# Seven half-block products instead of eight in the gate and up matmuls of four feed-forward blocks

## The chip, the core and the metric

The kernel runs on one core of a Trainium2 chip. TensorE (PE, with its weight loads as PEld) multiplies, VectorE (DVE) and ScalarE (ACT) work elementwise, GpSimd (POOL) does a little elementwise work and issues some transfers, and SyncE (SP) issues the others. The metric is the time of one execution in microseconds (us) on the device; lower is better. All inputs and outputs are fp32 in HBM.

## The reference, cut to what matters

Two transformer blocks follow each other on 512 tokens of width 1024 (528 tokens in the first feed-forward block, which has 16 meta tokens ahead). Each block has a feed-forward net, a mixer and a second feed-forward net; this case is about the four feed-forward nets.

```python
D_MODEL, D_FF = 1024, 2816

def rmsnorm(x, g):
    xf = x.astype(jnp.float32)
    y = xf * lax.rsqrt(jnp.mean(xf * xf, axis=-1, keepdims=True) + EPS)
    return (y * g.astype(jnp.float32)).astype(x.dtype)

def swiglu(x, w_in, w_out):
    gu = x @ w_in
    return (jax.nn.silu(gu[..., :D_FF]) * gu[..., D_FF:]) @ w_out

# first block, first net (the other three are alike, two without the outer norm)
h = h + 0.5 * rmsnorm(swiglu(rmsnorm(h, gn[0]), ffn_w_in[i, 0], ffn_w_out[i, 0]), gn[1])
```

## The kernel before, in words

**Numbers as pairs.** Every fp32 operand of a matmul is kept as a high and a low part (`hi`, `lo`, both fp32r). A product is three matmuls: hi by hi, hi by lo, lo by hi (function `mm`, line 366). The hidden state `h` is stored with features on the partitions: 8 blocks of 128 features by 528 tokens. `nh` and `nl` are the two parts of `h` times the norm's gain. The norm's factor per token, `r_bc`, is not in them: it is multiplied in after the matmul, when the result is taken out of PSUM.

**Gates and ups.** The 2816 hidden columns are 22 chunks of 128, done in three parts of 6, 8 and 8 (`PARTS`). A chunk is one `Item` of two units: the gate's weights and the up's weights, each 1024 by 128. `run_mm` runs 2 units x 8 feature blocks x 3 = 48 matmuls of 512 columns (in the first net two slices of 272 and 256 columns, so 96). `Ffn.evac` (lines 481 to 485, `split` at 347 and 348) then makes silu(gate) times up from the two PSUM tiles and stores it as the pair `gh`, `gl`. After each part `Ffn.down` multiplies by the output weights (tile `dn`), adding into `y` (or `h`); the last part's down is joined to the next stage in `Bridge.tail` in the first two nets.

**Weights.** `Weights` has a list of loads (`raws`) and of units to make of them (`subs`). `dma` loads one raw tile of 128x2048 fp32 by SP (line 77): for a chunk the gate's 512 KB and the up's 512 KB. There are two raw tiles. `pump` takes the next unit when a slot is free: ACT casts to fp32r (tile `whi`, line 96), DVE subtracts to get the low part (`wlo`, line 97; in the mixers POOL does it). There are six slots (`w4` with 4, `w2` with 2; four in the third net past its first chunks; in the last net `w4` and four of `wx`). A slot is free again when PE has used it, and a raw tile when its last unit is split.

**Order.** Each engine runs its own instructions strictly in the order in which the build leaves them; semaphores tie the engines together. The build's tile layer may shift neighbouring instructions from the order of the source.

**Rotary tables.** In the third net (`ffn3`), a set of some 25 DVE instructions (`tables`, line 1004) is placed in the middle of part 1; its positions are loaded by POOL at line 1002.

Of the kernel before, what the change touches and what calls it, by code (L numbers as in the profile page):

```python
# [15 lines left out]
P = 128  # L16
# [38 lines left out]

class Weights:


    def __init__(self, nc, raw_pool, raw_ahead):
        self.nc = nc  # L60
        self.raw_pool, self.raw_ahead = raw_pool, raw_ahead
        self.raws, self.subs, self.units = [], [], []
        self.raw_tiles = {}
        self.n_raw = self.n_split = self.n_take = self.n_free = 0
        self.pools = []
        self.lo_engine = nc.vector

    def add(self, loads, subs):
        r = len(self.raws)
        self.raws.append([loads, len(subs)])  # L70
        self.subs.extend((r, s) for s in subs)

    def dma(self, n):
        while self.n_raw < min(n, len(self.raws)):
            t = self.raw_pool.tile([P, 2048], F32, tag="raw", name="raw")
            for dst, src in self.raws[self.n_raw][0]:
                self.nc.sync.dma_start(out=dst(t), in_=src)
            self.raw_tiles[self.n_raw] = t
            self.n_raw += 1

    def pump(self):
        nc = self.nc
        while self.n_split < len(self.subs):
            room = [p for p in self.pools if p[1] > 0]
            if not room:
                break
            slot = max(room, key=lambda p: p[1])
            slot[1] -= 1
            pool = slot[0]
            r, make = self.subs[self.n_split]  # L90
            self.dma(r + 1)
            hi = pool.tile([P, 1024], F32R, tag="whi", name="whi")
            lo = pool.tile([P, 1024], F32R, tag="wlo", name="wlo")
            unit, splits = make(self.raw_tiles[r], hi, lo)
# [20 lines left out]

    def free(self, k):
        for _ in range(k):
            self.units[self.n_free].slot[1] += 1
            self.units[self.n_free] = None
            self.n_free += 1  # L120
        self.pump()

    def open(self, pool, n):
        self.pools.append([pool, n, n])

    def close(self, pool):
# [14 lines left out]
def two_blocks(ctx: ExitStack, tc, d, out):  # L141
# [13 lines left out]
    w4 = ctx.enter_context(tc.tile_pool(name="w4", bufs=4))  # L155
# [19 lines left out]
    def col(i):  # L175
        return vec[:, i:i + 1]
# [25 lines left out]

    def add_down(ap, f0, nf):
# [15 lines left out]
    def add_ffn(g_ap, g0, u_ap, u0, d_ap):  # L219
        for f0, nf in PARTS:  # L220
            for f in range(f0, f0 + nf):
                add_gu(g_ap, g0, u_ap, u0, f)
            add_down(d_ap, f0, nf)

    def add_gates(ap):
# [3 lines left out]
        def make(raw, hi, lo):  # L229
            src, hv, lv = view(raw), grid(hi, KD), grid(lo, KD)  # L230
# [234 lines left out]

    class Ffn:
        def __init__(self, name, half):
            self.cm, self.p = open_pool(name)
            self.half = half
# [6 lines left out]
        def evac(self, f, sl, g, u):  # L476
            t0, n = sl
            r = r_bc[:, t0:t0 + n]
            a = self.p.tile([P, 512], F32, tag="a", bufs=2, name="a")[:, 0:n]
            b = self.p.tile([P, 512], F32, tag="b", bufs=2, name="b")[:, 0:n]  # L480
# [5 lines left out]
            split(cut(self.gh, f, sl), cut(self.gl, f, sl), b)  # L486

# [30 lines left out]
    class Bridge:  # L518
# [24 lines left out]
        def tail(self, hl, nk, sink):  # L543
# [4 lines left out]
            cm, more = open_pool("w8", bufs=2, side="right")  # L548
# [39 lines left out]
    cm_w2, w2 = open_pool("w2", bufs=2)  # L588
# [3 lines left out]
    ffn = Ffn("ffn1", 0.5)  # L592
# [17 lines left out]
    W.open(w4, 4)  # L610
# [49 lines left out]
    for part in range(3):  # L660
        items = ffn.items(part)
        if part == 0:
            run_lead(items[:3], br)
            items = items[3:]
            p = ps("vt")
            pe.transpose(p[:, 0:P], vrow, ident)
            dve.tensor_copy(out=vec[:, 48:P], in_=p[:, 48:P])
            for i in (1, 5):
                g = vec[:, V_GN[i]:V_GN[i] + KD]
                dve.tensor_scalar(out=g, in0=g, scalar1=0.5, scalar2=None, op0=ALU.mult)  # L670
        for it in items:
            run_item(it, AB)
        if part < 2:
            ffn.down(PARTS[part][1], AB, sum_y(part == 0))
# [283 lines left out]
    run_lead(items[:3], br)  # L958
    for part in range(3):
        for it in items[3:] if part == 0 else ffn.items(part):  # L960
            run_item(it, [XF])
        if part < 2:
            ffn.down(PARTS[part][1], [XF], sum_y(part == 0))
# [18 lines left out]
    add_ffn(d["ffn2_w_gate_2"][0], 0, d["ffn2_w_up_2"][0], 0, d["ffn2_w_down_2"][0])  # L982
    br = Bridge(XA, XB, V_GN[5], V_F1)
# [6 lines left out]
    run_lead(items[:3], br)  # L990
    W.close(w2)
    for it in items[3:]:
        run_item(it, [XF])
    cm_t, trig = open_pool("trig", side="right")
# [3 lines left out]
    posi = trig.tile([P, 512], I32, tag="sqTrue", bufs=1, name="posi")  # L998
    sinR = trig.tile([P, SEQ], F32, name="sinR")
    cosR = trig.tile([P, SEQ], F32, name="cosR")  # L1000
    tabM = trig.tile([P, SEQ], F32, name="tabM")
    pool.dma_start(out=posi, in_=d["positions_2"][0].partition_broadcast(P))

    def tables():
        def tmp(tag):
            return ffn.p.tile([P, 512], F32, tag=tag, bufs=1 if tag == "th" else 2, name=tag)
        ang, n, k, z, q = tmp("a"), tmp("a"), tmp("b"), tmp("b"), tmp("th")
# [33 lines left out]
    for part in range(3):
        if part:
            for i, it in enumerate(ffn.items(part)):
                run_item(it, [XF])
                if part == 1 and i == 1:
                    tables()
        ffn.down(PARTS[part][1], [XF], add_h((lambda c: pre_chunk(c, XF, V_MIX, pre)) if part == 2 else None))
# [384 lines left out]
    cm_x, wx = open_pool("wx", bufs=4)  # L1432
    W.open(wx, 4)
    W.pump()
    for part in range(3):
        items = ffn.items(part)
        if part == 0:
            run_first(items[0], items[1], ONE, pre)
            items = items[2:]
        for it in items:  # L1440
            run_item(it, ONE)
        if part < 2:
            ffn.down(PARTS[part][1], ONE, add_h())
# [100 lines left out]
```

## Time and profile before

| what | value |
|---|---|
| median of three runs | 2133.37 us (2132.86 to 2138.08) |
| the profiled execution, its run | 2133.48 us |
| the profiled execution, its span | 2131.7 us |
| TensorE's granted clock over the span | 0.988 of full |
| PE busy, share of the span | 97% |
| DVE, ACT, POOL busy | 60%, 38%, 8% |
| HBM read | 180.20 MB, 87 GB/s over the span |

The span is the time from the first to the last instruction of the profiled execution; the run's own time lies 1.8 us above it. Busy time of PE is modelled from pipelined matmuls, so what counts is the time between starts. An engine that is off the chain of waits costs nothing while it idles.

### The profile page before, as it was taken

What the parts mean: (1) busy time and instruction counts of PE and PEld (TensorE: products, weight loads), DVE (VectorE), ACT (ScalarE), POOL (GpSimd) and SP (SyncE); (2) the same over time, 40 slices, a digit from 0 to 9 for tenths busy, and PEclk for the clock granted to TensorE, in tenths of its full rate; (3) what the DMA queues carried; (4) which work ended last, traced back from release to release, by engine and by line L of the source; (5) the groups of instructions that cost most, each with busy time, mean ns of one, the idle gap of its engine ahead of it and who ended that gap; (6) DMA issues with size and microseconds to landing.
All of it is one profiled execution on the core that took longest, in us unless ns stands there. A gap on an engine that the chain in (4) does not pass through costs nothing.

```text
span 2131.7 us, 29589 instructions
## 1 busy us (share of the span) xinstructions
PE 2073.6 (97%) x12047; PEld 1816.5 (85%) x12047; DVE 1278.3 (60%) x2217; ACT 813.7 (38%) x1365; POOL 161.5 (8%) x162
## 2 busy tenths in 40 slices
PE   8999999989999999999999999998999999999998
PEld 8999999988889988888998888887777778888888
DVE  6545345787886734444674653557888875454454
ACT  5333223335455433223342332334666643222222
POOL 0000000025440000000000000003222100000000
PEclk9999999989999999999999999999999999999999
DMA  5232322213322233223322333323212143333311
GB/s 160 92 110 80 100 85 86 70 55 90 95 80 86 64 109 99 91 88 99 93 82 78 99 99 99 99 82 92 56 41 65 40 132 105 100 99 99 99 60 40
DMA packets 285422, 186.32 MB, mean 87 GB/s; under 512 B 6332, under 2 KB 281527, under 8 KB 285287
## 3 DMA queue, kind: packets, MB, share of 16 engines
q1 hardware_dynamic: 282630, 176.15, 27.4%
q0 software_dynamic: 2096, 7.05, 1.0%
q8 instruction: 94, 1.54, 0.3%
q10 hardware_dynamic: 560, 1.24, 0.2%
q14 instruction: 42, 0.34, 0.0%
HBM read 180.20 MB, written 4.23 MB: 87 GB/s over the span
## 4 chain that ended last, share of the span: by engine, by line
PE 83%; DVE 10%; ACT 4%; issue 2%; POOL 1%; DMA 0%; ACTq 0%; POOLq 0%; DVEq 0%; SPq 0%
PE acc L366 46%; PE dn L366 24%; PE accB L366 3%; PE accA L366 3%; PE wo L366 2%; DVE accF L909 1%; PE p L301 1%; PE ro L1318 1%; ACT whi L96 1%; DVE cv L770 1%; DVE wlo L97 1%; PE p L333 1%; PE ms L1176 1%; DVE sl L348 1%; ACT mp L1185 0%
## 5 line engine op out<-in xcount | busy, mean ns | idle before, releaser
L96 ACT CAST whi<-raw 128x1024 fp32r<-128x1024 f32 (+4 forms) x350 | 345.9, 992 | 806.2 <-PE acc L366 488.2
L366 PE MATMUL acc<-nh,whi 128*128 128x512 f32 (+1 forms) x2000 | 639.5, 352 | 10.5 <-DVE y L915 5.6
L366 PE MATMUL acc<-nl,whi 128*128 128x512 f32 (+1 forms) x2000 | 637.2, 352 | 0.0
L366 PE MATMUL acc<-nh,wlo 128*128 128x512 f32 (+1 forms) x2000 | 635.3, 351 | 0.0
L366 PEld LDWEIGHTS acc<-nh,whi 128*128 128x128 f32 x2000 | 350.8, 189 | 65.2 <-DVE y L915 6.1
L97 DVE TENSOR_TENSOR wlo<-raw,whi 128x1024 fp32r<-128x1024 f32 (+1 forms) x293 | 347.0, 1186 | 85.3 <-ACT whi L96 84.5
L366 PEld LDWEIGHTS acc<-nh,wlo 128*128 128x128 f32 x2000 | 350.4, 190 | 51.4
L366 PEld LDWEIGHTS acc<-nl,whi 128*128 128x128 f32 x2000 | 349.2, 189 | 50.1
L366 PE MATMUL dn<-gh,whi 128*128 128x512 f32 (+2 forms) x1008 | 311.7, 328 | 0.1
L366 PE MATMUL dn<-gl,whi 128*128 128x512 f32 (+2 forms) x1008 | 311.7, 328 | 0.0
L366 PE MATMUL dn<-gh,wlo 128*128 128x512 f32 (+2 forms) x1008 | 310.8, 327 | 0.0
L482 DVE SCALAR_TENSOR_TENSOR b<-acc,r_bc 128x512 f32<-128x512 f32 (+1 forms) x98 | 56.1, 589 | 254.5 <-PE acc L366 254.5
L366 PEld LDWEIGHTS dn<-gh,whi 128*128 128x128 f32 x1008 | 181.6, 188 | 19.7 <-ACT gh L347 1.6
L366 PEld LDWEIGHTS dn<-gl,whi 128*128 128x128 f32 x1008 | 181.7, 188 | 18.2 <-DVE gl L348 0.6
L366 PEld LDWEIGHTS dn<-gh,wlo 128*128 128x128 f32 x1008 | 181.8, 188 | 17.0
L97 POOL TENSOR_TENSOR wlo<-raw,whi 128x1024 fp32r<-128x1024 f32 (+3 forms) x57 | 108.5, 1913 | 217.3 <-ACT whi L96 186.7
L481 DVE TENSOR_TENSOR a<-acc,r_bc 128x512 f32<-128x512 f32 (+1 forms) x98 | 56.1, 589 | 100.1 <-PE acc L366 100.0
L484 ACT ACTIVATE a<-a 128x512 f32<-128x512 f32 (+2 forms) x116 | 59.7, 532 | 81.9 <-DVE b L483 80.6
L347 ACT CAST gh<-b 128x512 fp32r<-128x512 f32 (+2 forms) x116 | 58.7, 520 | 82.7 <-DVE b L485 82.7
L348 DVE TENSOR_TENSOR gl<-b,gh 128x512 fp32r<-128x512 f32 (+2 forms) x116 | 63.7, 564 | 43.0 <-ACT gh L347 42.2
L1034 DVE TENSOR_TENSOR h<-dn,h 128x512 f32<-128x512 f32 x40 | 27.7, 692 | 98.6 <-PE dn L366 98.6
L582 DVE TENSOR_TENSOR y<-dn,y 128x256 f32<-128x256 f32 (+2 forms) x56 | 25.3, 464 | 75.1 <-PE dn L366 75.0
(327 smaller groups left out, 2565.5 us busy)
## 6 DMA issues: line engine op xcount, KB each, us to landing
raw<-in_ffn_w_in SPq DMA_DIRECT2D x88, 512.0 KB, 3.7
raw<-in_ffn_w_gate SPq DMA_DIRECT2D x44, 512.0 KB, 3.7
raw<-in_ffn_w_up SPq DMA_DIRECT2D x44, 512.0 KB
raw<-in_ffn_w_out SPq DMA_DIRECT2D x16, 1024.0 KB, 5.0
raw<-in_ffn_w_down SPq DMA_DIRECT2D x16, 1024.0 KB, 5.2
raw<-in_a_w_in SPq DMA_DIRECT2D x18, 512.0 KB, 3.9
raw<-in_w_in SPq DMA_DIRECT2D x16, 512.0 KB, 3.6
raw<-in_ffn_w_out SPq DMA_DIRECT2D x8, 768.0 KB, 4.3
```

What stands on the lines that cost most here:

```text
L96: nc.scalar.copy(out=ho, in_=src)
L97: self.lo_engine.tensor_tensor(out=lw, in0=src, in1=ho.bitcast(F32), op=ALU.subtract)
L301: pe.matmul(self.p1[:, self.n:self.n + 2], lhsT=src[:, o:o + P], rhs=ones[:, 0:2], start=True, stop=True)
L333: pe.matmul(p2[:, o:o + hi - lo], lhsT=ones, rhs=dg, start=True, stop=True)
L347: act.copy(out=hi, in_=src)
L348: dve.tensor_tensor(out=lo, in0=src, in1=hi.bitcast(F32), op=ALU.subtract)
L366: pe.matmul(p, lhsT=w[:, k], rhs=cut(x, k, sl), start=(k == 0 and j == 0), stop=(k == last and j == 2))
L481: dve.tensor_tensor(out=a, in0=g, in1=r, op=ALU.mult)
L482: dve.scalar_tensor_tensor(out=b, in0=u, scalar=self.half, in1=r, op0=ALU.mult, op1=ALU.mult)
L484: act.activation(out=a, in_=a, func=ACTF.Tanh, scale=0.5)
L582: dve.tensor_tensor(out=cut(y, c, sl), in0=p, in1=cut(y, c, sl), op=ALU.add)
L1034: dve.tensor_tensor(out=cut(h, c, sl), in0=p, in1=cut(h, c, sl), op=ALU.add)
```

## The change

Of each net's 22 chunks, the 16 of parts 1 and 2 are computed in another way; the 6 of part 0 stay as they were. Take the two halves of the 1024 features as rows and the two halves of the tokens as columns, and the gate's and the up's weights as two block rows: a chunk is then a 2x2 by 2x2 block product, which takes seven products of half size where the plain form takes eight (Strassen, in Winograd's form).

- **Products.** `Ffn.seven` runs seven products of 4 feature blocks x 3 = 12 matmuls, each with half of the tokens as columns (264 in the first net, 256 in the others). Two run with the gate's own halves (P1, P2), one with the up's second half (P4), four with sums of weight halves (P3, P5, P6, P7). They add up in three PSUM tiles, `sa`, `sb`, `sc`; intermediate sums are copied out on the way (`ht`, `rp`, `sqFalse`), since `sa` goes on growing. P4 and P3 of a chunk run inside the next chunk: PE's order is P1 P2 P4(old) P6 P3(old) P5 P7.
- **Input.** Sums of input halves need the norm's factor inside, so `Ffn.prepare` makes the normed input (`normed`, into `y`) and from it seven pairs: four of them lie in `nh`, `nl`, two in new tiles on the right side of SBUF, one in the reserved slot `wide`. The steps run beside the last two items of part 0 (in the last net the last three), `rest` after them.
- **Weights.** `add_seven` loads the gate (512 KB), the up's first half twice (256 KB each, once into the raw tile, once into a small tile `rawx`) and the second half once. Two transfers issued by POOL then add to what is there: the up's second half onto its first, and the gate's first half onto `rawx`. Two more sums are made by DVE. Units become `gates` (two halves), `three` (half a slot), `twos` (two halves), `ups` and `four` (half a slot each).
- **Slots.** One slot (`wide`) and the two of `w2` are taken out for this: three whole slots stay, and `w2` becomes four half slots.
- **Around it.** `evac` works in cuts of 256 columns. In the third net `tables` and its load move behind part 2's products, ahead of the last down.

```diff
     def dma(self, n):
         while self.n_raw < min(n, len(self.raws)):
+            loads, _, more = self.raws[self.n_raw]
             t = self.raw_pool.tile([P, 2048], F32, tag="raw", name="raw")
-            for dst, src in self.raws[self.n_raw][0]:
+            if more:
+                t = t, self.more.tile([P, 512], F32, tag="rawx", bufs=2, name="rawx")
+            for dst, src in loads:
                 self.nc.sync.dma_start(out=dst(t), in_=src)
+            for dst, src in more:
+                self.nc.gpsimd.dma_start(out=dst(t), in_=src, accum_op=ALU.add)
...
+    def add_seven(g_ap, g0, u_ap, u0, f):
...
+        def three(t, hi, lo):
+            x = t[0][:, 0:512]
+            dve.tensor_tensor(out=x, in0=x, in1=t[0][:, 1536:2048], op=ALU.add)
+            return cut_of(hi, lo, 1), [(hi, lo, x)]
+
+        def twos(t, hi, lo):
+            return cut_of(hi, lo, 2), [(hi[:, 0:512], lo[:, 0:512], t[0][:, 1536:2048]),
+                                       (hi[:, 512:1024], lo[:, 512:1024], t[1])]
...
+        def four(t, hi, lo):
+            x = t[0][:, 512:1024]
+            dve.tensor_tensor(out=x, in0=x, in1=t[0][:, 0:512], op=ALU.add)
+            return cut_of(hi, lo, 1), [(hi, lo, x)]
...
+        W.add([(lambda t: grid(t[0][:, 0:1024], 8), rows(g_ap, g0, 0, 2)), (part(3), rows(u_ap, u0, 0)),
+               (other, rows(u_ap, u0, 0)), (part(2), rows(u_ap, u0, 1))], [gates, three, twos, ups, four],
+              halves=(1, 3, 4), more=[(part(3), rows(u_ap, u0, 1)), (other, rows(g_ap, g0, 0))])
...
+    def run_ffn(ffn, items, slices, down, halves, gcol, xn, spare, close_w2=False, before=None):
...
+        run_item(items[0], slices)
+        slots += [W.reserved.pop(0) for _ in range(3 - len(slots))]
+        steps, rest = ffn.prepare(halves, gcol, xn, slots)
+        todo, did = items[1:], 0
+        for i, it in enumerate(todo):
+            upto = len(steps) * (i + 1) // len(todo)
+            run_item(it, slices, steps=steps[did:upto])
+            did = upto
...
+        rest()
+        down(0)
...
+        for part in (1, 2):
+            ffn.seven(range(PARTS[part][1]))
+            if part == 1:
+                down(1)
...
+            steps = [lambda k=k: normed(k) for k in range(KD)]
+            steps += [lambda: split(*b11, x11), lambda: split(*b21, x21),
+                      lambda: dve.tensor_tensor(out=x11, in0=x11, in1=x12, op=sub),
+                      lambda: dve.tensor_tensor(out=x12, in0=x22, in1=x12, op=sub)]
+            steps += [lambda k=k: second(k) for k in range(4)]
+
+            def rest():
+                for dst, src in ((t1, x11), (t3, x12), (t4, x21), (b22, x22)):
+                    split(*dst, src)
...
+            def up_a(o):
+                self.product(o.a, o.u2, 0, "P4")
+                dve.scalar_tensor_tensor(out=o.s1, in0=o.a, scalar=-self.half, in1=o.s1, op0=ALU.mult, op1=ALU.mult)
+                split(self.gh[:, o.f, ta:ta + n], self.gl[:, o.f, ta:ta + n], o.s1)
+                W.release(o.u2)
+
+            def gate_b(o):
+                self.product(o.c, o.u4, 0, "P3")
+                g, t = yt("sqFalse", n), self.tmp("b", n)
+                dve.tensor_tensor(out=g, in0=o.c, in1=o.m2, op=ALU.add)
+                act.activation(out=t, in_=g, func=ACTF.Tanh, scale=0.5)
+                dve.scalar_tensor_tensor(out=g, in0=t, scalar=1.0, in1=g, op0=ALU.add, op1=ALU.mult)
+                dve.scalar_tensor_tensor(out=g, in0=o.c22, scalar=-self.half, in1=g, op0=ALU.mult, op1=ALU.mult)
+                split(self.gh[:, o.f, tb:tb + n], self.gl[:, o.f, tb:tb + n], g)
+                W.release(o.u4)
+
+            old = None
+            for f in fs:
...
+                (u,) = W.take(1)
+                o.a, b = ps("sa")[:, 0:n], ps("sb")[:, 0:n]
+                self.product(o.a, u, 0, "P1", True)
+                m1 = yt("ht", n)
+                act.copy(out=m1, in_=o.a)
+                self.product(b, u, 1, "P2", True)
+                o.s1, t = self.tmp("a", n), self.tmp("b", n)
+                dve.tensor_tensor(out=o.s1, in0=b, in1=m1, op=ALU.add)
+                act.activation(out=t, in_=o.s1, func=ACTF.Tanh, scale=0.5)
+                W.release(u)
+                if old:
+                    up_a(old)
+                dve.scalar_tensor_tensor(out=o.s1, in0=t, scalar=1.0, in1=o.s1, op0=ALU.add, op1=ALU.mult)
+                (u,) = W.take(1)
+                self.product(o.a, u, 0, "P6")
+                o.m2 = yt("rp", n)
+                act.copy(out=o.m2, in_=o.a)
+                W.release(u)
+                if old:
+                    gate_b(old)
+                (u,) = W.take(1)
+                o.c = ps("sc")[:, 0:n]
+                self.product(o.c, u, 0, "P5", True)
+                self.product(o.a, u, 1, "P7")
+                m3 = yt("sqFalse", n)
+                act.copy(out=m3, in_=o.a)
+                o.c22 = yt("sqacc", n)
+                dve.tensor_tensor(out=o.c22, in0=o.c, in1=m3, op=ALU.add)
+                W.release(u)
+                o.u2, o.u4 = W.take(2)
+                old = o
+            up_a(old)
+            gate_b(old)
```

**DVE's order, one chunk of the second net.** Before: the five instructions that take a chunk out of PSUM and the two low parts of its weights.

```order
L481 TENSOR_TENSOR a_8926<-acc_8876,r_bc_83 128x512 [waits PE_49]
L97 TENSOR_TENSOR wlo_8936<-raw_8873,whi_8935 128x1024 [waits DMAHW2_49,Activation_49]
L482 SCALAR_TENSOR_TENSOR b_8927<-acc_8877,r_bc_83 128x512 [waits PE_49]
L483 TENSOR_TENSOR b_8927<-a_8926,b_8927 128x512 [waits DVE_49]
L97 TENSOR_TENSOR wlo_8940<-raw_8873,whi_8939 128x1024 [waits DMAHW3_49,Activation_49]
L485 SCALAR_TENSOR_TENSOR b_8927<-a_8926,b_8927 128x512 [waits Activation_49]
L348 TENSOR_TENSOR gl_7651<-b_8927,gh_7650 128x512 [waits Activation_49]
```

The same net after, 11 of a chunk's 17 rows, from the gates' low part on. `raw_8892` is the raw tile of the chunk that is running, `raw_9025` that of the next one; L285 is the sum in `three`, and the last but one row is the low part of `four` of the running chunk, the last reader of `raw_8892`. DMASW waits are waits for the adding transfers of POOL.

```order
L109 TENSOR_TENSOR wlo0_105<-raw_9025,whi0_104 128x1024 [waits DMAHW6_49,PE_49,Activation_49]
L737 TENSOR_TENSOR sqacc_8973<-sc_8946,sqFalse_8971 128x256 [waits Activation_49]
L285 TENSOR_TENSOR raw_9025<-raw_9025 128x512 [waits DMASW4_49,DVE_49]
L717 TENSOR_TENSOR a_9003<-sb_8976,ht_8989 128x256 [waits PE_49,Activation_49]
L109 TENSOR_TENSOR wlo1_107<-raw_9025,whi1_106 128x512 [waits Activation_49]
L722 SCALAR_TENSOR_TENSOR a_9003<-b_9004,a_9003 128x256 [waits Activation_49]
L691 SCALAR_TENSOR_TENSOR a_8870<-sa_8842,a_8870 128x256 [waits PE_49]
L109 TENSOR_TENSOR wlo1_107<-rawx_9026,whi1_106 128x512 [waits DMASW1_49]
L452 TENSOR_TENSOR gl_7635<-a_8870,gh_7634 128x256 [waits Activation_49]
L109 TENSOR_TENSOR wlo1_115<-raw_8892,whi1_114 128x512
L109 TENSOR_TENSOR wlo1_115<-raw_9025,whi1_114 128x512 [waits PE_49,Activation_49]
```

The next chunk's sum, which waits for an adding transfer, now stands ahead of the running chunk's own rows and of the last reader of its raw tile. The last reader is seven rows behind the sum here; in every second chunk of the last three nets it is three rows behind it (in the first net six and five in turn).

**POOL's order, the same place.** Before it has no row here. After, two adding transfers per chunk, `rawx` ahead of the raw tile of the same time:

```order
L93 DMA rawx_9026<-in_ffn_w_in 128x4x128 [waits DMASW7_49,DMASW1_49,DMAHW1_49,DVE_49,Activation_49]
L93 DMA raw_8892<-in_ffn_w_in 128x4x128 [waits DMASW5_49,DMAHW3_49,DVE_49,Activation_49]
L93 DMA rawx_9159<-in_ffn_w_in 128x4x128 [waits DMAHW5_49,DMASW0_49,DVE_49]
L93 DMA raw_9025<-in_ffn_w_in 128x4x128 [waits DMAHW4_49,DMAHW7_49,DMASW6_49,DVE_49]
L93 DMA rawx_9292<-in_ffn_w_in 128x4x128 [waits DMASW1_49,DMAHW1_49,DVE_49,Activation_49]
```

Each waits for the load by SP of the bytes that it adds to (DMAHW).

**ACT's order, the end of a part.** Before, the end of a chunk: the tanh and the high part of the result, then the next casts.

```order
L484 ACTIVATE a_9454<-a_9454 128x512 [waits DVE_49]
L347 CAST gh_7650<-b_9455 128x512 [waits DVE_49]
L96 CAST whi_9533<-raw_9471 128x1024 [waits DMAHW0_49,PE_49,Activation_49]
L96 CAST whi_9537<-raw_9471 128x1024 [waits DMAHW1_49,PE_49,Activation_49]
L484 ACTIVATE a_9524<-a_9524 128x512 [waits DVE_49]
```

After, the last chunk of part 1 in the second net. L735 is the copy of P7's sum, after which P4 may add to the same PSUM tile; `raw_9563` is the second load of the down weights.

```order
L108 CAST whi0_112<-raw_9424 128x512 [waits PE_49]
L451 CAST gh_7634<-a_9402 128x256 [waits DVE_49]
L726 COPY rp_9578<-sa_9507 128x256 [waits PE_49]
L700 ACTIVATE b_9593<-sqFalse_9592 128x256 [waits DVE_49,Activation_49]
L451 CAST gh_7634<-sqFalse_9592 128x256 [waits DVE_49]
L108 CAST whi1_106<-raw_9563 128x1024 [waits DMAHW7_49,PE_49]
L735 COPY sqFalse_9625<-sa_9507 128x256 [waits PE_49,Activation_49]
L451 CAST gh_7634<-a_9535 128x256 [waits DVE_49]
```

The cast of a down unit, which waits for its load, stands ahead of the copy that P4 waits for; this is so at the end of all eight parts.

## Rows read from the trace of the kernel before

**Rows 1.** The page: busy time by engine, and the chain's shares.

```profile
PE 2073.6 (97%) x12047; PEld 1816.5 (85%) x12047; DVE 1278.3 (60%) x2217; ACT 813.7 (38%) x1365; POOL 161.5 (8%) x162
PE 83%; DVE 10%; ACT 4%; issue 2%; POOL 1%; DMA 0%; ACTq 0%; POOLq 0%; DVEq 0%; SPq 0%
```

**Rows 2.** The chain of waits in time: start us, length us, what, count.

```profile
128.13 93.43 PE acc L366 x768
...
800.28 89.02 PE acc L366 x384
889.30 44.62 PE dn L366 x192
...
2088.18 5.65 PE dn L366 x48
```

**Rows 3.** Windows: eight chunks of the last net; busy us (count), PEclk, DMA share, GB/s.

```profile
1850.40:1939.30 88.90, 88.90 (x385) 72.05 (x385) 43.96 (x53) 25.54 (x31) 0.00 (x0) 1.00 0.30 95
```

**Rows 4.** Groups by form: line, engine, operation, tiles, shape, count | busy us, mean ns.

```profile
L97 DVE TENSOR_TENSOR wlo<-raw,whi 128x1024 fp32r<-128x1024 f32 x258 | 315.0, 1222 | 77.3 <-ACT whi L96 76.4 <-issue 0.7
L96 ACT CAST whi<-raw 128x1024 fp32r<-128x1024 f32 x299 | 313.0, 1049 | 725.3 <-PE acc L366 431.1 <-PE dn L366 220.3 <-issue 29.4
...
L348 DVE TENSOR_TENSOR gl<-b,gh 128x512 fp32r<-128x512 f32 x60 | 41.5, 692 | 39.2 <-ACT gh L347 39.2
...
L347 ACT CAST gh<-b 128x512 fp32r<-128x512 f32 x60 | 37.2, 621 | 60.2 <-DVE b L485 60.2
...
L485 DVE SCALAR_TENSOR_TENSOR b<-a,b 128x256 f32<-128x256 f32 x34 | 14.2, 419 | 1.2 <-ACT a L484 1.1
...
L347 ACT CAST gh<-b 128x256 fp32r<-128x256 f32 x34 | 13.8, 406 | 4.1 <-DVE b L485 4.1
...
L580 ACT COPY y<-dn 128x256 f32<-128x256 f32 x24 | 8.8, 371 | 9.7 <-PE dn L366 9.6
```

**Rows 5.** Timeline, second net: start us, length us, engine, line, operation.

```profile
823.32 0.69 DVE L483 TENSOR_TENSOR b<-a,b 128x512 f32<-128x512 f32 x1
823.93 1.22 DVE L97 TENSOR_TENSOR wlo<-raw,whi 128x1024 fp32r<-128x1024 f32 x1
...
825.07 0.68 DVE L485 SCALAR_TENSOR_TENSOR b<-a,b 128x512 f32<-128x512 f32 x1
825.18 1.08 SPq L77 DMA_DIRECT2D raw<-in_ffn_w_in  x2
```

**Rows 6.** Timeline of DVE, three 256-wide instructions in a dense stretch.

```profile
720.75 0.41 DVE L482 SCALAR_TENSOR_TENSOR b<-accA,r_bc 128x256 f32<-128x256 f32 x1
721.08 0.41 DVE L481 TENSOR_TENSOR a<-accA,r_bc 128x256 f32<-128x256 f32 x1
721.41 0.41 DVE L483 TENSOR_TENSOR b<-a,b 128x256 f32<-128x256 f32 x1
```

**Rows 7.** Transfers, window 820:836 in 40 slices: what was moved in each.

```profile
GB/s 0 0 0 0 0 0 0 0 20 0 0 0 0 0 0 36 99 252 347 361 332 335 348 348 214 12 0 0 0 0 0 0 0 0 0 0 0 0 0 0
```

**Rows 8.** Transfers, whole span: issuing queue, count, KB each, median us from issue to landing.

```profile
raw<-in_ffn_w_in SPq DMA_DIRECT2D x88, 512.0 KB, 3.7
...
raw<-in_ffn_w_out SPq DMA_DIRECT2D x16, 1024.0 KB, 5.0
...
Abc<-AEd POOLq DMA_DIRECT2D x8, 256.0 KB, 3.3
...
posi<-in_positions POOLq DMA_DIRECT2D x1, 256.0 KB, 5.0
```

More of the change, by code (lines that the diff above doesn't have):

```diff
@@ L83, in pump @@
         while self.n_split < len(self.subs):
[L84 to L85 removed]
+            r, make, half = self.subs[self.n_split]
+            idle = self.idle_halves if half else self.idle
+            if not idle:
                 break
[L87 to L90, printed above, removed]
+            slot = idle.pop(0)
             self.dma(r + 1)
[L92 to L94 removed]
+            unit, splits = make(self.raw_tiles[r], slot.hi, slot.lo)
             for ho, lw, src in splits:
@@ L659, in two_blocks @@
     AB = [A_SL, B_SL]
[L660 to L674, printed above, removed]
+    items = ffn.items(0)
+    run_lead(items[:3], br, "wide")
+    p = ps("vt")
+    pe.transpose(p[:, 0:P], vrow, ident)
+    dve.tensor_copy(out=vec[:, 48:P], in_=p[:, 48:P])
+    for i in (1, 5):
+        g = vec[:, V_GN[i]:V_GN[i] + KD]
+        dve.tensor_scalar(out=g, in0=g, scalar1=0.5, scalar2=None, op0=ALU.mult)
+    run_ffn(ffn, items[3:], AB, lambda part: ffn.down(PARTS[part][1], AB, sum_y(part == 0)),
+            [(0, TT // 2), (TT // 2, TT // 2)], V_GN[0], y, None)
     br = Bridge(A_SL, B_SL, V_GN[1], V_GN[2])
@@ L957, in two_blocks @@
     items = ffn.items(0)
[L958 to L963, printed above, removed]
+    run_lead(items[:3], br, "wide")
     add_ffn(d["ffn1_w_gate_2"][0], 0, d["ffn1_w_up_2"][0], 0, d["ffn1_w_down_2"][0])
@@ L989, in two_blocks @@
     items = ffn.items(0)
[L990 to L1002, printed above, removed]
+    run_lead(items[:3], br, "wide")
     def tables():
-        def tmp(tag):
-            return ffn.p.tile([P, 512], F32, tag=tag, bufs=1 if tag == "th" else 2, name=tag)
-        ang, n, k, z, q = tmp("a"), tmp("a"), tmp("b"), tmp("b"), tmp("th")
+        ang, n, k, z, q = [y[:, i, 0:SEQ] for i in range(5)]
         magic = 12582912.0
@@ L1037, in add_h @@
         return sink
+    run_ffn(ffn, items[3:], [XF], lambda part: ffn.down(PARTS[part][1], [XF], add_h()), [XA, XB], V_F1, y, None, True)
+    W.close(w2)
+    cm_t, trig = open_pool("trig", side="right")
+    posi = trig.tile([P, 512], I32, tag="sqTrue", bufs=1, name="posi")
+    sinR = trig.tile([P, SEQ], F32, name="sinR")
+    cosR = trig.tile([P, SEQ], F32, name="cosR")
+    tabM = trig.tile([P, SEQ], F32, name="tabM")
+    pool.dma_start(out=posi, in_=d["positions_2"][0].partition_broadcast(P))
+    tables()
     sq.update(pool=trig, bufs=1)
     pre = Rms(XF)
[L1041 to L1047, printed above, removed]
+    ffn.down(PARTS[2][1], [XF], add_h(lambda c: pre_chunk(c, XF, V_MIX, pre)))
     ffn.close()
```

192 lines of the change are left out of this document (156 added, 36 removed).

## The prediction

> **What bounds the kernel now.** I read the page first: PE is busy 97% of the span and holds 83% of the chain, DVE 60%, ACT 38% [rows 1]. Then the chain in order of time: a part of eight chunks is one piece of PE work without a break, 93.43 us for 768 matmuls in the first net and 89.02 us for 384 in the others [rows 2]. The windows say the same of the last net: PE busy 88.90 of 88.90 us at a granted clock of 1.00 (the 2.4 GHz level), while DVE works 43.96 us, or 5.50 per chunk, and ACT 25.54 [rows 3]. So in these stretches only fewer or cheaper matmuls give time, and DVE, ACT and the transfers have room. The question is how much of it the change uses up.
>
> **PE: what is taken away.** In nets 2 to 4 a chunk takes 89.02 / 8 = 11.13 us, 231.8 ns per 512-wide matmul. The final down runs 256-wide: 48 in 5.65 us, 117.7 ns each [rows 2], so half the width is nearly half the price. The new chunk is 7 x 12 = 84 of them: 9.89 us, 1.24 less. In the first net a matmul of 264 columns on average takes 93.43 / 768 = 121.7 ns, so 11.68 becomes 84 x 0.1217 = 10.22, 1.46 less. Sum: 48 x 1.24 + 16 x 1.46 = 82.9 us. All of it is on the path.
>
> The trace shows 231.8 ns at 512 columns and 117.7 at 256. The Trainium skill (TensorE: Matmul & The Clock Gate, "Back-to-back issue gap") gives about 131 ns at 512 and 81 at 128 for a sustained stream with its weight loads, which speaks against halving the width: an estimate between them, 98 ns at 256, would make 8.2 us of a chunk where 6.3 were, a loss. The trace does not agree, and the measurement decides.
>
> **DVE and ACT: what is added.** Before, DVE splits 2 x 1024 columns of weights per chunk; now 1024 and five times 512, with two sums of 512 beside it: 1.22 + 7 x 0.69 = 6.06 us. The products are taken out with nine 256-wide instructions of 0.42: 3.77. That is 9.84 us against 9.89 of PE, from 5.50. But independent instructions start closer than they last: 512 columns after 0.61 us, 1024 after 1.14 [rows 5], 256 after 0.33 [rows 6]. By starts it is 1.14 + 7 x 0.61 + 9 x 0.33 = 8.4. ACT has 1.05 + 5 x 0.62 of casts, four 256-wide casts and tanhs of 0.41 and three copies of 0.37 [rows 4]: 6.9. Both fit, just; they have about 1.5 us a chunk to lose in waits for each other. The walk through a chunk at PE's pace comes out even: from the end of P3 to the copy of P7's sum (cast 0.62, low part 0.61, sum 0.61, sum of the gate 0.33, low part 0.69, two dependent steps of 0.45, cast 0.41, cast of the next gates 1.05, copy 0.37) is 5.6 us, and the three products from P4 to P3 are 4.2: 9.8.
>
> **Transfers: the ring that I expect to bind.** Two raw tiles are there. A raw tile is loaded again when `four` of its chunk is split. Then SP loads gate and up (it issues 0.03 us after the reader ended, 823.93 + 1.22 to 825.18 [rows 5]); POOL waits for the first 768 KB to land and issues the add; and the sum in `three`, which waits for that, stands on DVE ahead of the `four` that frees the other tile (the order of DVE above). What is queued behind that waiting sum on DVE is the running chunk's own work, and on ACT the cast that waits for the same transfer holds back the copy of P6's sum, without which P7 can't start. So one turn of the ring is load + add + rows of DVE, and it must be done in a chunk's 9.89 us.
>
> Load: 1.05 MB issued at 825.18 was through at about 829.9 [rows 7] at some 345 GB/s; 768 KB are through 0.8 us sooner, and with the signal it is 4.2 us (512 KB land after 3.7, 1024 after 5.0 [rows 8]). DVE from the sum to `four`, by starts: eight rows in 4.0 us (0.61 + 0.33 + 0.61 + 0.38 + 0.33 + 0.61 + 0.40 + 0.69), four rows in 2.4. The add is not in the trace: no transfer there adds. Nearest are POOL's plain transfers of the same 256 KB, 3.3 us (eight of them), and the slowest of that size, 5.0 [rows 8]. Below 3.3 I see nothing that an add would save. I take 4.2: 3.3 and another 0.8 for reading the 256 KB that are added to at 345 GB/s.
>
> A part has five turns that can bind (the first two chunks are loaded beside the down before): two with eight rows and three with four. With 4.2 + 4.2 = 8.4 that is 5 x 8.4 + 2 x 4.0 + 3 x 2.4 = 57.2 us where PE wants 5 x 9.89 = 49.5. The first 1.3 us cost nothing, as P7 has that much room for its copy. Excess 6.4 per part, 38.7 in six parts; in the first net (six and five rows, 15.8 in place of 15.2; PE 51.1) 5.4 per part, 10.8. Sum **49.5 us**. With 3.3 for the add it is 13.5, with 5.0 it is 81.5. Bandwidth itself does not bind: 1.75 MB per chunk is some 180 GB/s, twice the 95 of [rows 3] and half of 345.
>
> **The end of a part.** The last P4 follows P7 at once, with no P1 and P2 between. It waits for the copy of P7's sum, and that stands on ACT behind the cast of a down unit that waits for its 1 MB (order of ACT above). That load starts when the last `four` is split, about 7.4 us into the chunk (P4 ends at 4.2; then casts, tanh and the low part of a down unit), lands 5.0 later [rows 8], then cast 1.05 and copy 0.37 [rows 4]: 13.9 where P7 ended at 9.9. **4.1 us, eight times: 33.** If the load is not late, 1.5 each (12); if DVE is late, up to 5.4 (43).
>
> **Making the input.** DVE's steps are eight of 0.69, four of 1.22 and twelve of 0.42: 15.4 us, and `rest` 4.9 more. The last two chunks of part 0 hold 22.3 us and 11.0 of DVE already, so 4.1 hang over into the down, and ACT's casts of `rest` stand ahead of the last chunk's tanh. The down's first unit reads that chunk only at its 16th matmul, 15 x 0.232 = 3.5 us later [rows 2]. I take 2.5 us per net, **10** in all (0 to 24). In the third net `tables` (some 12 us of DVE) stands ahead of the last down; eight PSUM banks of 5.6 us each cover its sums, and only the low parts of down weights can be late: **3** (0 to 12).
>
> **Sum.** Against the profiled execution (span 2131.7, run 2133.5, 0.1 from the median): 2133.5 - 82.9 + 49.5 + 33 + 10 + 3 = **2146 us**, +0.6%. The saving is real and is spent on waits: the ring takes most of it.
>
> **The rivals.**
> - *The add is quick* (faster). If it lands as a plain transfer does, 3.3 us, the ring takes 13.5 and the time is 2110; below 2.6 the turn is as long as PE's chunk and the ring takes nothing: 2133.5 - 82.9 + 46 = 2097. It decides from an add of 3.7 us downward (2127). For it: the eight transfers of 3.3; against: an add has to read twice. Beside it, the Trainium skill (DMA: Bandwidth & Descriptors, "Anatomy of one DMA — SWDGE (gpsimd) path") puts a transfer from POOL at 2.0 us and the bytes at 436 GB/s, an estimate of 2.6 for 256 KB and so 2097; the trace has 3.3 for that size, and the same page's rules for authors say that an adding transfer reads its destination and writes it later. Chance 0.28.
> - *PE's pace holds throughout*: the turns and the ends of parts are covered, since DVE runs by starts and the loads come early; ends of parts 12, input 0 to 10: 2133.5 - 82.9 + 12 + 5 + 3 = 2071. For it: DVE's 8.4; against: both orders above, which put a waiting row ahead of what PE needs. Chance 0.10.
> - *DVE is the bound.* If its rows cost what they last, 9.84, and it waits for one cast of 0.41 and the gates' 1.05 in each chunk, a chunk takes 11.3: 64 x 1.4 = 90 in place of the ring's 49.5, 2187. It decides where the waits pass 1.5 us a chunk. Against: in the dense stretch starts are 0.33 apart where 0.41 is the length [rows 6]. Chance 0.12.
>
> **How the numbers follow.** The forecast with adds of 3.7 to 5.0 us has 0.50 and spans 2127 to 2178. About 0.3% is what a measurement of this kernel can tell from no change: 2127 to 2140. Of the 0.50, 0.14 lies there (adds of 3.7 to 4.1) and 0.36 above. Faster: 0.28 + 0.10 = 0.38. Same: 0.14. Slower: 0.36 + 0.12 = 0.48. The range takes in both ends of the add and most of the quick rival and leaves out the last of the third and of the fourth: 2085 to 2180.
>
> **What would show it.** PE's chunks: 84 matmuls in 9.9 us with no gap in the first two chunks of each part, then gaps of 1 to 2 us ahead of P7, ended by ACT's copy `rp`, with the sum at L285 on DVE and the cast of `twos` on ACT waiting for `raw` from POOL. A landing of POOL's adds near 4.2 us. A gap of about 4 us ahead of the last P4 of each of eight parts, ended by the copy `sqFalse`. DVE busy near 8.5 us per chunk. If POOL's adds land in 3.3 us or less, or if the rows at L285 never wait, the ring is wrong; if PE waits for DVE while no transfer is late, the fourth case is right; if 256-wide products take more than 118 ns back to back, the first term is.

## The result and the profile after

The changed kernel takes 2215.7 us (median of four runs, 2208.2 to 2222.4) against 2134.1: 1.038 times the time of before, 95% interval 1.034 to 1.041. The forecast was 2146 with a range to 2180; the time lies above it, on the side that was held likeliest and much further out. The profiled execution has a span of 2206.4 us, 74.7 above the one of before, and all sums below are made against these two.

The page of the changed kernel, busy time and chain, to be set beside [rows 1]:

```profile
PE 2036.7 (92%) x13583; PEld 1865.0 (85%) x13583; DVE 1537.7 (70%) x2949; ACT 1025.6 (46%) x1973; POOL 326.3 (15%) x290
PE 43%; DMA 18%; DVE 13%; ACT 6%; issue 4%; POOL 1%; SPq 0%; POOLq 0%; ACTq 0%; DVEq 0%
```

PE held 83% of the chain and now holds 43%; transfers held nothing and hold 18%. No engine is full: DVE went from 60% to 70% and PE fell. So things wait for each other.

Where: the windows of two parts with eight seven-product chunks each, second net part 1 and last net part 1. Columns are start and end, length, busy time and count of PE, PEld, DVE, ACT, POOL, then granted clock, DMA share and GB/s; [rows 3] are those of before.

```profile
811.51:915.24 103.73, 86.60 (x679) 83.94 (x678) 66.30 (x127) 48.44 (x100) 17.97 (x14) 0.97 0.66 146
1906.23:2006.85 100.62, 85.84 (x679) 82.81 (x678) 67.14 (x128) 47.77 (x99) 17.97 (x14) 0.98 0.68 151
```

These parts took 89.0 us and take 103.7 and 100.6, while DVE works 66 and 67 of them. Over the eight parts it is 809.0 us where before had 720.7: 88 us more, and everything outside of them 13.6 less (some 11 of which are only a few matmuls of the next down, 1.4 us or a little more, that now run inside each part's end). The loss is in these parts and nowhere else.

What waits there: PE's waits and DVE's, summed (engine, line, waited for, us in total, times, longest).

```profile
PE sa L680 <- ACT rp L726: 81.0, 40, 3.7
PE sa L680 <- ACT sqFalse L735: 28.9, 30, 2.1
...
DVE raw L285 <- DMA raw<-in_ffn_w_in: 68.5, 20, 4.1
DVE raw L285 <- DMA raw<-in_ffn_w_up: 68.4, 21, 4.7
```

Forty waits for the copy `rp`, ahead of P7, and forty-one of the sum at L285 for the added-up tile: eight parts with five binding turns each, the number that the prediction counted. The copy `sqFalse` in the second line is that of P7's sum; on ACT it stands behind the cast of the next gates, which waits for their load (1.56 us at 858.59, ahead of the copy at 859.54). One turn of the ring, as the chain of waits gives it in the second net (start us, length us, what):

```profile
867.41 0.37 SPq L91
867.78 0.05 issue
867.83 5.13 DMA raw<-in_ffn_w_in
...
873.03 0.48 issue
...
873.53 4.72 DMA raw<-in_ffn_w_in
...
878.27 0.63 ACT whi L108
...
878.95 0.42 DVE a L717
879.37 0.60 DVE wlo L109
879.97 0.34 DVE a L722
880.30 0.34 DVE a L691
...
882.24 5.13 DMA raw<-in_ffn_w_in
```

Load, add, and the rows of DVE and ACT from the waiting sum to the next load; no piece of PE is in it. It lasts 14.8 us where PE needs 9.9. Over the forty binding turns the mean is 13.65 us: 5.75 from the first issue of the load to POOL's issue of the add, 4.92 from there to the sum, 2.98 from the sum to the next load. The same place on the timeline of DVE and ACT, one chunk earlier, shows why the turn closes:

```profile
865.09 0.62 ACT L108 CAST whi<-raw 128x512 fp32r<-128x512 f32 x1 [4.39 <-DMA raw<-in_ffn_w_in]
865.16 0.69 DVE L285 TENSOR_TENSOR raw<-raw 128x512 f32<-128x512 f32 x1 [3.60 <-DMA raw<-in_ffn_w_in]
865.77 0.68 DVE L109 TENSOR_TENSOR wlo<-rawx,whi 128x512 fp32r<-128x512 f32 x1
...
865.93 0.60 ACT L108 CAST whi<-raw 128x512 fp32r<-128x512 f32 x1
866.37 0.42 DVE L691 SCALAR_TENSOR_TENSOR a<-sa,a 128x256 f32<-128x256 f32 x1
866.70 0.68 DVE L109 TENSOR_TENSOR wlo<-raw,whi 128x512 fp32r<-128x512 f32 x1
```

The row at 866.70 is the low part of `four` of the chunk before: the last reader of the other raw tile. It stands behind a sum that waits 3.60 us for an add. Moving it ahead on DVE alone would not free the tile: the cast that it needs, at 865.93, stands on ACT behind the cast of `twos`, which waits 4.39 us for the same add. (The rows do not name the tile; in the next run, where the sum lies in `accF`, the row `whi<-accF` has this place in ACT's order.) So two engines hold the tile back, where the prediction told of DVE alone.

### The profile page after: what moved, and what is told of

Its sections match the earlier page's. It is cut to its first block, busy times and chain, and to the rows that moved or that the text cites. A ratio compares the mean times of both kernels' runs of the same rounds, so it can differ in the third digit from the quotient of the medians.

```text
span 2206.4 us, 34988 instructions
## 1 busy us (share of the span) xinstructions
PE 2036.7 (92%) x13583; PEld 1865.0 (85%) x13583; DVE 1537.7 (70%) x2949; ACT 1025.6 (46%) x1973; POOL 326.3 (15%) x290
## 4 chain that ended last, share of the span: by engine, by line
PE 43%; DMA 18%; DVE 13%; ACT 6%; issue 4%; POOL 1%; SPq 0%; POOLq 0%; ACTq 0%; DVEq 0%
PE dn L470 19%; PE acc L470 10%; DMA raw<-in_ffn_w_up 7%; DMA raw<-in_ffn_w_in 6%; DVE wlo L109 3%; ACT whi L108 3%; PE sa L680 2%; PE accB L470 2%; DMA raw<-in_ffn_w_down 2%; PE wo L470 2%; PE accA L470 2%; DMA raw<-in_ffn_w_out 2%; DMA raw<-in_ffn_w_gate 2%; PE sc L680 1%; DVE accF L1161 1%
## 5 line engine op out<-in xcount | busy, mean ns | idle before, releaser
L108 ACT CAST whi<-raw 128x512 fp32r<-128x512 f32 (+3 forms) x500 | 396.9, 799 | 519.1 <-PE dn L470 188.0
L109 DVE TENSOR_TENSOR wlo<-raw,whi 128x512 fp32r<-128x512 f32 (+2 forms) x456 | 408.3, 906 | 146.9 <-ACT whi L108 143.4
L470 PE MATMUL dn<-gh,whi 128*128 128x256 f32 (+2 forms) x908 | 277.4, 326 | 0.4 <-ACT gh L451 0.4
L470 PE MATMUL dn<-gl,whi 128*128 128x256 f32 (+2 forms) x908 | 277.6, 326 | 0.0
L470 PE MATMUL dn<-gh,wlo 128*128 128x256 f32 (+2 forms) x908 | 277.2, 325 | 0.0
L680 PE MATMUL sa<-nh,whi 128*128 128x256 f32 (+1 forms) x488 | 150.9, 309 | 102.5 <-ACT rp L726 73.6
L470 PE MATMUL acc<-nh,whi 128*128 128x512 f32 (+2 forms) x600 | 195.8, 360 | 9.2 <-DVE z L1009 4.0
L470 PE MATMUL acc<-nl,whi 128*128 128x512 f32 (+2 forms) x600 | 191.3, 354 | 0.0
L470 PE MATMUL acc<-nh,wlo 128*128 128x512 f32 (+2 forms) x600 | 190.7, 353 | 0.0
L470 PEld LDWEIGHTS dn<-gh,wlo 128*128 128x128 f32 x908 | 163.2, 188 | 14.8
L680 PE MATMUL sa<-nh,wlo 128*128 128x256 f32 (+1 forms) x488 | 143.7, 294 | 0.0
L285 DVE TENSOR_TENSOR raw<-raw 128x512 f32<-128x512 f32 x64 | 44.2, 691 | 137.2 <-DMA raw<-in_ffn_w_in 68.5
```

The lines of the kernel that those rows point to most:

```text
L108: nc.scalar.copy(out=ho, in_=src)
L109: self.lo_engine.tensor_tensor(out=lw, in0=src, in1=ho.bitcast(F32), op=ALU.subtract)
L285: dve.tensor_tensor(out=x, in0=x, in1=t[0][:, 1536:2048], op=ALU.add)
L470: pe.matmul(p, lhsT=w[:, k], rhs=cut(x, k, sl), start=(k == 0 and j == 0), stop=(k == last and j == 2))
L680: pe.matmul(acc, lhsT=w[:, 4 * i + k], rhs=x[:, k], start=start and k == 0 and j == 0, stop=k == 3 and j == 2, skip_group_check=not start)
```

## Experiments

**The ring cut.** The sum that `four` takes is written into `accF`, a tile that is idle in these stretches, instead of over half of the raw tile. The raw tile is then free when this sum and the low part of `ups` are done, and both stand ahead of the waiting sum on DVE; no cast that they need stands behind the waiting one on ACT.

```diff
         def four(t, hi, lo):
-            x = t[0][:, 512:1024]
-            dve.tensor_tensor(out=x, in0=x, in1=t[0][:, 0:512], op=ALU.add)
+            x = accF
+            dve.tensor_tensor(out=x, in0=t[0][:, 512:1024], in1=t[0][:, 0:512], op=ALU.add)
```

> Only the place of the sum G11+G21 changes: DVE writes it into the tile accF, so the raw tile is free when that sum is taken and not when its low part is. On DVE this stands ahead of the waiting sum at L285 of the next chunk, so load, add and DVE rows of two chunks no longer follow each other in one ring. Theory ring of two raw tiles: the waits ahead of P6 and P7 go, the eight parts fall from 809 us to 8 x 672 products of half blocks at 118 ns (122 in the first net) and some 2.9 us at each end, 662 us: the run is 2061 us (2050 to 2085). Rival transfers: load 5.2 and add 4.9 us per chunk are queued work of their own that takes over 9.9 us whatever tile is free: 2190 to 2215, unchanged. Rival DVE: its rows set the chunk, at 11 us or more: 2150 or more.

Measured: 2057.1 us (four runs, 2056.7 to 2057.8), 0.963 times the kernel before, interval 0.962 to 0.965. Both rivals are out. Page and windows of it, the two parts named first above and the last part of the last net:

```profile
PE 1995.2 (97%) x13583; PEld 1838.1 (89%) x13583; DVE 1541.1 (75%) x2949; ACT 1041.2 (51%) x1973; POOL 326.4 (16%) x290
PE 80%; DVE 11%; ACT 4%; issue 2%; DMA 2%; POOL 1%; SPq 0%; POOLq 0%; ACTq 0%; DVEq 0%
```

```profile
778.07:858.95 80.88, 80.88 (x680) 80.37 (x678) 66.36 (x127) 49.13 (x100) 17.97 (x14) 1.00 0.85 185
1791.05:1873.35 82.30, 81.41 (x679) 80.69 (x678) 67.52 (x128) 50.01 (x99) 17.99 (x14) 1.00 0.85 184
1916.52:1998.15 81.63, 81.63 (x688) 81.50 (x687) 69.34 (x129) 52.34 (x100) 15.10 (x12) 1.00 0.73 162
```

The granted clock is 1.00, and PE is busy without a break in two of the three, with 0.9 us idle in the other; the part that took 103.73 us takes 80.88. DVE does the same 66 us of work, now beside PE. The transfers carry the same bytes in less time (185 GB/s), so bandwidth was not the limit either. The timeline of it, second net, one chunk's stretch, rows of SP, DVE and POOL:

```profile
804.75 2.06 SPq L91 DMA_DIRECT2D raw<-in_ffn_w_in  x3
...
808.46 0.68 DVE L285 TENSOR_TENSOR raw<-raw 128x512 f32<-128x512 f32 x1
...
811.59 0.68 DVE L109 TENSOR_TENSOR wlo<-accF,whi 128x512 fp32r<-128x512 f32 x1
...
812.47 1.28 POOL L93 DMA_DIRECT2D raw<-in_ffn_w_in  x1 [4.93 <-DVE wlo L109]
```

The sum no longer waits, and the low part of `four` still stands behind it, but it reads `accF` and holds no raw tile. The load at 804.75 has its add at 812.47 and its sum at 818.14. That is 13.4 us from load to sum, longer than in the ring, and it costs nothing, since the next load goes out at 814.44 without waiting for it. DVE's sum at L285 waits twice in the whole run (1.9 and 2.0 us) instead of 41 times.

**The adds left out.** Both adding transfers of a chunk go; `three` and the tile `rawx` stay. From here on each time is that of one run, to be set beside the 14 us over which the changed kernel's own four runs spread.

```diff
-            if more:
+            if more is not ():
                 t = t, self.more.tile([P, 512], F32, tag="rawx", bufs=2, name="rawx")
...
-               (other, rows(u_ap, u0, 0)), (part(2), rows(u_ap, u0, 1))], [gates, three, twos, ups, four],
-              halves=(1, 3, 4), more=[(part(3), rows(u_ap, u0, 1)), (other, rows(g_ap, g0, 0))])
+               (other, rows(u_ap, u0, 0)), (part(2), rows(u_ap, u0, 1))], [gates, three, twos, ups, four], halves=(1, 3, 4), more=[])
```

> The two adding transfers of every chunk are left out (so the sums U11+U21 and U11+G11 lack their second term); order and everything else stay. Theory ring: a turn is load and DVE rows, 5.2 + 2.3 to 3.9 = 7.5 to 9.1 us, less than the 9.9 of PE, so no turn binds: 2050 to 2085 us. Rival DVE: the rows are the same, so the time stays above 2150. Rival load alone too slow: gaps of PE ended by the load, 2100 or more.

Measured: 2098.1 us. The expectation of PE's pace was missed, by 13 us from its upper end and 41 from the cut kernel: the ring still binds, though by less. The timeline of one turn, SP, ACT and DVE:

```profile
838.90 1.63 SPq L91 DMA_DIRECT2D raw<-in_ffn_w_in  x3
...
843.66 1.04 ACT L108 CAST whi<-raw 128x1024 fp32r<-128x1024 f32 x1 [1.42 <-DMA raw<-in_ffn_w_in]
...
844.74 1.23 DVE L109 TENSOR_TENSOR wlo<-raw,whi 128x1024 fp32r<-128x1024 f32 x1 [2.04 <-ACT whi L108]
...
846.21 0.68 DVE L285 TENSOR_TENSOR raw<-raw 128x512 f32<-128x512 f32 x1
...
850.11 0.37 SPq L91 DMA_DIRECT2D raw<-in_ffn_w_out  x1
```

The turn is 11.2 us, the mean of the forty 10.9, where PE needs 9.9. The gates' cast and low part, which come first out of the tile and stand ahead of the sum, ran beside the add before; without it they are in the ring, 4.8 to 7.3 us after the load's issue. The model of the turn as load, add and rows left them out, since the add covers them. No DVE bound shows: DVE's rows are as many, and it waits for ACT, which waits for the load. The third case, the load alone too slow, comes near: PE's longest waits in sum are the 33 for the copy `sqFalse` (30.2 us), which stands on ACT behind that cast of the gates. But it is the load with the rows behind it that make the turn, not the load alone.

**Plain transfers in place of adding ones.** The instruction order is the same in every row.

```diff
-                self.nc.gpsimd.dma_start(out=dst(t), in_=src, accum_op=ALU.add)
+                self.nc.gpsimd.dma_start(out=dst(t), in_=src)
```

> POOL's adding transfers become plain ones of the same bytes to the same place (the second term replaces the first). The order of all instructions is the same. If adding is what makes them 4.9 us long, they take 3.3 us as the plain ones of that size did in the kernel before, and 40 binding turns give 64 us: 2144. If it is POOL's way of sending, or the traffic beside it, they stay at 4.6 to 5.0 us and the time at 2195 to 2215.

Measured: 2144.6 us, on the number of the first case. POOL's transfers of 256 KB (queue, count, KB each, median us from issue to landing), the two lines of the changed kernel and, in the second fence, of this one:

```profile
raw<-in_ffn_w_in POOLq DMA_DIRECT2D x32, 256.0 KB, 4.8
...
raw<-in_ffn_w_up POOLq DMA_DIRECT2D x32, 256.0 KB, 4.8
```

```profile
raw<-in_ffn_w_in POOLq DMA_DIRECT2D x32, 256.0 KB, 3.3
...
raw<-in_ffn_w_up POOLq DMA_DIRECT2D x32, 256.0 KB, 3.2
```

Adding costs 1.5 us per transfer, and each binding turn is shorter by about that: in the last two nets 13.46 us become 12.05, of which 4.90 and 3.38 are the time from the add's issue to the sum. The same two transfers with the ring cut:

> The sum in accF, as in e1_sum_elsewhere, and the adding transfers plain, as in e3_plain_transfers (the second term replaces the first). In the uncut ring the plain ones gave 64 us. Theory ring: with the ring cut the add has room, so its length no longer counts: 2057 as in e1_sum_elsewhere, within 6 us. Rival: the add itself stands on the path in every chunk whatever the tiles do, and the cut only took the DVE rows out of it: then the shorter transfer gives another 30 us or more, 2027 or less.

Edit: the two diffs above together. Measured: 2054.4 us, 2.7 below the cut alone, inside the 6 us that were allowed. What gave 64 us in the ring gives next to nothing outside of it. The length of the add counted because it stood in a ring, not because it stood anywhere near PE.

**The up's half loaded first.** The load's share of a turn was 5.8 us where 4.2 were forecast. Two runs ask why.

```diff
-        W.add([(lambda t: grid(t[0][:, 0:1024], 8), rows(g_ap, g0, 0, 2)), (part(3), rows(u_ap, u0, 0)),
-               (other, rows(u_ap, u0, 0)), (part(2), rows(u_ap, u0, 1))], [gates, three, twos, ups, four],
+        W.add([(part(3), rows(u_ap, u0, 0)), (other, rows(u_ap, u0, 0)),
+               (lambda t: grid(t[0][:, 0:1024], 8), rows(g_ap, g0, 0, 2)), (part(2), rows(u_ap, u0, 1))], [gates, three, twos, ups, four],
```

> Of each chunk's loads U11 goes out first and the gates after it; bytes are the same. If the add starts when its own 256 KB are there, the load's share of a turn falls from 5.2 to some 3.7 us and 40 turns give 60 us: 2148 (less where the gates then come late). If the adds wait for the whole tile, or the time of a turn is traffic and not order, 2195 to 2215.

Measured: 2199.9 us, little moved, though not for the reason that the second case gives. One turn in the third net:

```profile
1366.66 0.37 SPq L91 DMA_DIRECT2D raw<-in_ffn_w_up  x1
...
1370.72 1.74 POOL L93 DMA_DIRECT2D raw<-in_ffn_w_up  x1
...
1371.69 1.05 ACT L108 CAST whi<-raw 128x1024 fp32r<-128x1024 f32 x1 [1.06 <-DMA raw<-in_ffn_w_gate]
...
1376.69 0.62 ACT L108 CAST whi<-raw 128x512 fp32r<-128x512 f32 x1 [3.67 <-DMA raw<-in_ffn_w_up]
...
1378.28 0.68 DVE L285 TENSOR_TENSOR raw<-raw 128x512 f32<-128x512 f32 x1
...
1380.30 0.37 SPq L91 DMA_DIRECT2D raw<-in_ffn_w_up  x1
```

The add does start sooner, 4.0 us after the load on the mean instead of 5.8. But from the add to the sum it is now 6.4 us instead of 4.9: here 5.97 until the cast that waits for the added tile, and 1.59 more before the sum, which the build has set behind that tile's low part. So the order of the loads is worth 1.8 us at one place of the ring and nearly all of it is spent at the next. How much of the 6.4 is the other add, sent 0.85 us ahead in this turn, and how much the changed order on DVE, these runs don't separate. PE's waits move too: 26 of them, 40.0 us, are now for the copy `ht` of P1's sum, which stands on ACT behind the cast of the gates that come later.

**One add less.** The add into `rawx` travels while the next load does; it alone is left out.

```diff
-              halves=(1, 3, 4), more=[(part(3), rows(u_ap, u0, 1)), (other, rows(g_ap, g0, 0))])
+              halves=(1, 3, 4), more=[(part(3), rows(u_ap, u0, 1))])
```

> Of the two adding transfers of a chunk, the one into rawx is left out (so U11+G11 lacks G11); the one into raw, which stands in the ring, stays. What is asked is why the load's share of a turn is 5.2 to 6.2 us where 4.2 was forecast. If the other add's bytes, which travel at the same time, slow the load, it falls to 4.2 to 4.7 us and 40 turns of some 1.0 us give 40 us: 2165 (2150 to 2180). If the load is long by itself (three issues of SP and the signal), it stays near 5.3 and the time at 2190 to 2210.

Measured: 2208.1 us, no change, and turns of 13.51 us in the last two nets against 13.46. The other add's traffic does not lengthen the load. What is in the 5.8 us then: the up's half is the second of three loads, issued 0.42 us after the first (867.41 and 867.83 in the chain above), it lands 5.13 later there (median 4.4 to 4.5 for the up's loads), and POOL's transfer starts 0.57 after that (872.96 to 873.53). Why the landing takes 5.13 us is left open; the load into `rawx`, another 256 KB, goes out 0.93 us ahead of the first (866.48), and no run takes it away.

## Why the prediction was wrong, step by step

The sum of the prediction was 2133.5 - 82.9 + 49.5 + 33 + 10 + 3 = 2146. The cut kernel separates its terms, as it differs from the changed one in the ring, and in what the ring makes late at the ends of parts: spans 2131.7 before, 2055.7 cut, 2206.4 changed. Saving and all that stays with the ring cut: -76.0. Ring, with those ends: +150.7.

- **PE's saving, 82.9: right.** In the cut kernel a part of the second net is 80.88 us; less the six down matmuls of 1.39 us it is 79.5 for 672 products, 118.3 ns each, where 117.7 was taken from [rows 2]; over the run that is a few us less saved. The rule of the Trainium skill (TensorE: Matmul & The Clock Gate, "Back-to-back issue gap") that spoke against halving the width, 81 ns at 128 columns and 131 at 512, is not borne out here a second time.
- **The ring: right mechanism, a third of its size.** This is the step that failed. Place, DVE's order, the count of five binding turns in a part, and the rows of DVE (2.98 us measured, 15.2 / 5 = 3.04 forecast) were as told. Load and add were not: 5.75 + 4.92 = 10.7 us instead of 4.2 + 4.2 = 8.4. Forty turns, each 2.2 us longer than forecast, are 88 us. The prediction also let the first 1.3 us of every part go free, 10 us; the trace shows no such credit. With 49.5 that is 148, and the turns themselves give 147: 40 x 13.65 = 546 us, where PE wants 399.
- **The add, 4.2 forecast, 4.9 measured.** It lies next to the upper bound of 5.0 us, the one plain transfer of [rows 8] that was slowest; the value was taken nearer to the plain 3.3 with 0.8 for reading what is added to. The trace of plain ones (3.3) and adding ones (4.8) side by side puts the extra at 1.5. The Trainium skill (DMA: Bandwidth & Descriptors, "Rules for kernel authors") says that an adding transfer reads its destination and writes it later; the extra agrees in sign with that, and the page has no duration for it.
- **The load, 4.2 forecast, 5.8 measured.** This is the larger part, 62 us of the 88, and it was given no bounds at all. 4.2 was worked out from the bytes of one dense stretch in [rows 7]. It counted the gates' bytes ahead of the up's half, but not that the half, as the second of three issues, goes out 0.42 us later, nor that POOL sends half a microsecond after the landing that it waits for, which no row of the prediction showed.
- **The ends of parts, 33; the input, 10; tables, 3: too high by 35 us together.** In the changed kernel PE stands still for 0.3 to 2.0 us ahead of the last P4 of a part, 10.8 in the eight (from PE's timeline); with the 147 of the ring that is 158. The span lies 74.7 + 82.9 = 157.6 us above what the saving alone would give, so nothing is left for the input and the tables. In the cut kernel all three, with what the products take beyond 117.7 ns, are 82.9 - 76.0 = 6.9. The prediction's own terms for an end add up to 13.8 where it writes 13.9, so 3.9 an end and 31 in all. It said that the last P4 follows P7 at once. PE's timeline at an end in the changed kernel (second net) and in the cut one shows six matmuls of the down in between (6 to 14 at the other ends, some of them narrower):

```profile
909.34 0.40 PE L470 MATMUL dn<-gh,whi 128*128 128x512 f32 x1
...
910.51 0.39 PE L470 MATMUL dn<-gh,wlo 128*128 128x512 f32 x1
912.33 0.39 PE L680 MATMUL sa<-nh,whi 128*128 128x256 f32 x1 [1.44 <-ACT sqFalse L735]
```

```profile
854.57 0.40 PE L470 MATMUL dn<-gh,whi 128*128 128x512 f32 x1
...
855.73 0.39 PE L470 MATMUL dn<-gh,wlo 128*128 128x512 f32 x1
856.02 0.38 PE L680 MATMUL sa<-nh,whi 128*128 128x256 f32 x1
```

  In the changed kernel P4 starts 3.0 us after P7 is done, of which the six cover 1.4; in the cut one, where the down's load also finds its tile earlier, they cover all but a few hundredths. The wait is there, as told; the filler was overlooked. The input costs nothing that shows: the down of part 0, into which its last steps were to hang over, takes 33.4 us in the second net and 33.7 before.
- **The chances.** The quick add, 0.28, asked for 3.7 us or less; e3_plain_transfers shows what it would have given with plain transfers: 2144.6, not 2110, since the load too was longer than assumed. The DVE bound, 0.12, is out: 66 us of work in a part that PE can do in 80.9, and the cut kernel runs at PE's pace. "PE's pace holds", 0.10, gave 2071; with one sum written elsewhere the kernel does that and more, 2057. The range ended at 2180, the add's upper bound with the load's single value. With an upper bound for the load too, the 5.0 us of a 1024 KB load in [rows 8], the same sum gives 10 us a turn, 113 us of ring and 2210: about the profiled execution's 2208, if not the median. That nearness would be luck: the 46 us for ends, input and tables are 35 too high in it, and the credit of 1.3 us a part is kept. The add's upper bound was lucky as well: the row of 5.0 us in [rows 8] reads 3.4 to 3.7 in the later runs.

## What to carry to other kernels

When a buffer is reloaded in a ring, price the whole turn (issue, landing, the next engine's start, every instruction that stands between the waiting reader and the buffer's last reader, on each in-order engine that reads the buffer), and give every term of it bounds, since an error is paid once per turn. Then look for the last reader: writing one sum to another tile took it out of the ring and was worth 150 us, while making the same transfers shorter by a third was worth 64 in the ring and 3 outside of it. Halving the width of these fp32r matmuls costs about 2% per column (231.8 ns at 512 columns, 118.3 at 256), so that a saving of one product in eight is real where DVE and the loads keep up.

## What the runs showed of the hardware that was not expected

An adding transfer of 256 KB from POOL takes 4.8 us where a plain one to the same place takes 3.3.

TensorE's granted clock falls in the changed kernel's parts, and not in the cut kernel's. Three windows of one microsecond, in the second net, after PE had waited 2.2 us and then worked for 0.9 us (columns as above):

```profile
869.00:870.00 1.00, 1.00 (x7) 1.00 (x6) 1.00 (x3) 0.31 (x1) 0.00 (x0) 0.50 0.70 194
870.00:871.00 1.00, 1.00 (x7) 1.00 (x7) 1.00 (x3) 0.11 (x1) 0.91 (x1) 0.50 1.06 314
871.00:872.00 1.00, 1.00 (x6) 1.00 (x6) 0.53 (x3) 0.41 (x1) 0.37 (x1) 0.50 1.10 331
```

At 0.50, the 1.2 GHz level, a 256-wide product starts every 0.21 us instead of 0.118. Over the whole run PE is busy 41.5 us longer in the changed kernel than in the cut one with the same 13583 matmuls (2036.7 and 1995.2), and idle 109.2 us longer (169.7 and 60.5); the two make the 150.7. No piece of PE lies in the turns of the chain, so the slower products fill time that the ring takes anyway. No run here takes the clock alone away, but e3_plain_transfers speaks for this: its eight parts have a granted clock of 1.00 throughout, and its turns are shorter than the changed kernel's by 1.48 us on the mean, no more than the 1.55 by which the time from the add's issue to the sum is.

The times of the changed kernel spread over 0.6%, those of the cut one over 0.05%: that the scatter of the transfers on the path makes the difference is a guess, which no run tests.
